# Norm roots by a GpSimd power, and attention heads as three-stage units in a new order, in a two-block transformer kernel

## The chip, the cores and the metric

The kernel runs on one core of one Trainium2 chip. The metric is device time in microseconds (us) of one execution, inputs already in HBM. The core has TensorE (PE, with PEld for its weight loads), VectorE (DVE), ScalarE (ACT), GpSimd (POOL) and SyncE (SP), which issues most of the transfers. Each engine works through its own list of instructions in order.

## What is computed

256 tokens of width 1024 pass two blocks. The first has two layers of: SwiGLU feed-forward, layer norm, hybrid mixer, layer norm, SwiGLU feed-forward, layer norm. The mixer is the part that the change rewrites:

```python
h = split_columns(x @ w_in)                 # 2516 columns for the four mixers
y_a = mla_mixer(...)                        # M: 4 heads, low-rank queries and keys
y_b = nsa_mixer(...)                        # N: 4 heads x (compressed, selected, window)
y_c = dsa_mixer(...)                        # D: top 64 keys by an index score, 4 heads
y_d = stick_breaking_mixer(...)             # S: 4 heads, cumulative sum of log(1 - p)
y = rms_norm(concat(y_a, y_b, y_c, y_d) in 4 groups of 256, group_norm_g)
return y @ w_out
```

The second block (convolution, differential attention, and twice a layer that mixes 16384 experts by product keys) takes the rest of the time, and of it the change touches only the roots of the norms.

## The kernel before

**Layout and products.** Activations lie transposed, 128 of the 1024 features by 256 tokens in a tile. Every large product is made of three passes (`mm3`, L420 to L422): weights and activations are split into a high part in fp32r and the rest, and high by high, high by low and low by high are added in PSUM. `weights` (L391 to L398) brings 128x1024 pieces from HBM by SP, and for each 128x512 half ACT copies the high part (`wh`, L396) and VectorE or GpSimd subtracts it (`wl`, L398). `self.lo` is a string of engines taken in turn; in the mixers it is 'ggv' (two of three on GpSimd), at the head of a mixer or feed-forward `HEAD_LO`, 'g'. The ring has 4 raw pieces and 6 halves of each kind.

**Norms.** A residual sum `x` is written chunk by chunk in `project`, with running sums s1 and s2. `Rows.factors` reduces them with four small matmuls (L300, L301), makes mean and variance (L304 to L306), calls `newton` (L434 to L439: two integer instructions for a first guess and three rounds of three, eleven on VectorE), and `spread` (L445) lays the factors along the rows by PE transposes. So that PE need not wait for this, six input chunks of the mixer (EARLY), or four pairs of the feed-forward, are first computed from the unnormalised sum and corrected later (`normed`). `Rows.finish` then normalises: two VectorE instructions (L324, L325), ACT writes the high part (L328), GpSimd the full value (L329), VectorE the low part (L330). `newton` is also called by the norms inside the mixers (`mla_norm`, and `group_out`, once for each of the four groups) and by those of the second block, 30 times in all.

**Heads.** A head of M, N or D runs through `softmax`: `scores` (L762 and mask matmuls L764, L765, into PSUM bank B), row maxima (L775) and their negative (L777, or L779) on VectorE, exponent on ACT (L782), for N a gate on VectorE (L786, L788), three PE transposes (L791), a copy out of PSUM (L794 on ACT or L796 on VectorE), and then `pv` (L802 to L804), three matmuls into bank D. S has two passes, with all logarithms (L1056) between them. After four heads `group_out` squares, takes the root, scales, transposes (L750) and splits the result (L753, L754).

**Order.** `MIX_ORDER` names the steps, one letter each: b, i, n, d, c, 1, 2 and so on are input chunks and preparations, a and s score and select for D, and M, N, D and S each run one head whole. The layer's order ends `...SSSSSMMMMzsMsknnDDDDNNNNNNDNNNN`. These letters give priorities only: when the program is built, a scheduler fixes each engine's list from them and from estimated durations, and may move an instruction up where its buffers are free. The output product, `project` on `w_out`, follows all heads, eight chunks of 24 matmuls, with the groups in the order in which they end.

Of the kernel before, what the change touches and what calls it, by code (L numbers as in the profile page):

```python
# [15 lines left out]
U32 = mybir.dt.uint32  # L16
# [15 lines left out]
HEAD_LO = 'g'  # L32
HEAD_AT = 1
MIX_LO = ('ggv', 'ggv')
OUT_LO = ('ggv', 'ggv')
FFN_LO = 'v'
MIX_Z = ((), ())
MIX_BANKS = ('A', 'A')
EARLY = 0, 1, 2, 3, 5, 6
MIX_ORDER = ('1bbiciSbvbaaaS2paSduwSdSSSSSMMMMzsMsknnDDDDNNNNNNDNNNN', '1bbiciSbvbaaaS2paSduwSdSSSSSMMMMzsMsnnDDDDkNNNNNNDNNNN')  # L40
# [145 lines left out]
def _layout1(I):  # L186
# [11 lines left out]
    A['w_out'] = _chunked(I['w_out']).reshape(DEPTH, DC, 128, DC * 128)  # L198
# [86 lines left out]
class Rows:  # L285
# [8 lines left out]
    def factors(self, k):  # L294
# [12 lines left out]
        r = k.newton(v)  # L307
# [7 lines left out]
    def finish(self, k):  # L315
# [6 lines left out]
        for c in range(DC):  # L322
# [24 lines left out]
class Kernel:  # L347
    def __init__(self, ctx, nc, tc, I):
# [9 lines left out]
        nc.vector.memset(self.ones, 1.0)  # L358
        self.col = self.tl(gp, [128, 3], "col")
# [69 lines left out]
    def newton(self, v):  # L429

        nc = self.nc
        y = self.tl(self.wk, [128, 8], "ny", bufs=4)[:v.shape[0], :v.shape[1]]
        a = self.tl(self.wk, [128, 8], "na", bufs=4)[:v.shape[0], :v.shape[1]]
        nc.vector.tensor_scalar(y.bitcast(U32), v.bitcast(U32), 1, None, op0=ALU.logical_shift_right)  # L434
        nc.vector.tensor_scalar(y.bitcast(I32), y.bitcast(I32), -1.0, float(0x5f3759df), op0=ALU.mult, op1=ALU.add)
        for _ in range(3):
            nc.vector.tensor_tensor(a, v, y, op=ALU.mult)
            nc.vector.scalar_tensor_tensor(a, a, -0.5, y, op0=ALU.mult, op1=ALU.mult)
            nc.vector.scalar_tensor_tensor(y, a, 1.5, y, op0=ALU.add, op1=ALU.mult)  # L439
        return y  # L440
# [115 lines left out]
    def project(self, src, y, x, scale, eps, gb, out=None, order=None):  # L556
# [14 lines left out]
        for d in range(DC):  # L571
            w = self.weights(src[d], nk)
            ps = self.bank("ACD"[d % 3], T)
            self.linear(ps, w, y, order)
# [45 lines left out]
    def _mixer(self, ctx, l, sm, vec, now, dump):  # L620
# [16 lines left out]
        nf = [0]  # L637

        def fbank(cols):
            nf[0] += 1  # L640
            return self.bank(MIX_BANKS[l][nf[0] % len(MIX_BANKS[l])], cols)

        def fchunk(i, tag=None):

            if i in early:
                t = self.tl(mx, [128, T], tag) if tag else self.tl(mx, [128, 384], "p", bufs=3)[:, :T]
                now.normed(self, t, early[i])
                return t
            z = i in MIX_Z[l]
            ps = fbank(T + 2 if z else T)  # L650
            self.linear(ps, self.weights(win[i], DC), now.z if z else xs)
            if z:
                t = self.tl(mx, [128, T], tag) if tag else self.tl(mx, [128, 384], "p", bufs=3)[:, :T]
                now.normed(self, t, ps)
                return t
            return self.evac(ps, tag) if tag else ps

        def vchunk(name, n, tag):
            w = self.weights(I[name][l], DC, n)
            o = self.tl(mx, [128, 2, n], tag)  # L660
            for t, a in enumerate(TILES):
                ps = fbank(n)
# [7 lines left out]
        def features(n, tag, *chunks):  # L670

            E[n] = []
            for i in chunks:
                E[n].append(fchunk(i, f"{tag}{i}") if tag == "sb" else rope64(i, f"{tag}{i}") if tag == "nq" else rope32(i, f"{tag}{i}"))
                yield

        def once(f):
            f()
            yield
# [29 lines left out]
        def step_u():  # L709
# [4 lines left out]
        later = {  # L714
            'i': lambda: features('iq', "iq", 5, 6), 'n': lambda: features('nq', "nq", 8, 9),
            'd': lambda: features('dq', "nq", 10, 11), 'b': lambda: features('sb', "sb", 12, 13, 14, 15),
            'a': lambda: self.dsa_scores(acc, E['iq'], E['ik'], E['V']), 's': lambda: self.dsa_select(sel, acc),
            'M': lambda: self.mla(E['qkv'], E['kpe']), 'S': lambda: self.stick(E['sb'], lambda: E['sv']),
            'N': lambda: self.nsa(E['nq'], *E['kv'], (E['kk'], E['kx']), (E['kx'], E['kk']), E['V']),
            'D': lambda: self.dsa(E['dq'], (E['m2'], E['m2x']), E['V'], sel),  # L720
            **{n: (lambda f: lambda: once(f))(f) for n, f in zip("c12pwvkzu", (
                step_c, step_1, step_2, step_p, step_w, step_v, step_k, step_z, step_u))}}
        going = {}
        order = MIX_ORDER[l]
        for s in order:
            if s not in going:
                going[s] = later[s]()
            next(going[s], None)
        last = sorted('MNDS', key=order.rindex)

        self.lo = OUT_LO[l]
        return self.project(I['w_out'][l], self.ys, now.x, ALPHA, 1e-5, vec(V_L2G, 16), order=sum([[2 * g, 2 * g + 1] for g in map('MNDS'.index, last)], []))

    def group_out(self, grp, o):
# [9 lines left out]
        r = self.newton(ss)  # L744
        y = self.tl(self.mx, [128, 2, T], "y", bufs=2)
        ps = self.bank("C").rearrange("p (c t) -> p c t", c=2)
        for qc, a in enumerate(TILES):
            nc.vector.tensor_scalar(y[:, qc], o[:, qc], r[:, qc:qc + 1], None, op0=ALU.mult)
            for c in range(2):
                nc.tensor.transpose(ps[:, c, a], y[:, qc, c * 128:c * 128 + 128], self.id1)  # L750
        for c in range(2):
            g, (h, l) = self.vec1(V_GN + 2 * grp + c), self.ys[2 * grp + c]
# [15 lines left out]
    def softmax(self, s, scale, sums, rows=None, eng="v", gate=None):  # L768

        nc, C = self.nc, self.C  # L770
        mm = nc.tensor.matmul
        R = ((0, 128), (128, 384))
        st = self.tl(self.st, [128, 4], "st", bufs=8)
# [6 lines left out]
        p = self.tl(self.mx, [128, 384], "p", bufs=3)  # L780
# [3 lines left out]
        if gate is not None:  # L784
            self.recip(sums)
            nc.vector.tensor_tensor(sums, sums, gate, op=ALU.mult)  # L786
            for qc, (a, b) in enumerate(R):
                nc.vector.tensor_scalar(p[:, a:b], p[:, a:b], sums[:, qc:qc + 1], None, op0=ALU.mult)  # L788
        pt = self.bank("C", 384)
        for i in range(3):  # L790
            nc.tensor.transpose(pt[:, 128 * i:128 * i + 128], p[:, 128 * i:128 * i + 128], self.id1)  # L791
        o = self.tl(self.mx, [128, 384], "pt", bufs=3)
        if eng == "s":
            nc.scalar.activation(o, pt, AF.Copy)  # L794
        else:
            nc.vector.tensor_copy(o, pt)  # L796
        return o

    def pv(self, o0, o1, pt, v, start, stop):
# [11 lines left out]
    def heads(self, g, parts, v, scale, rows=None, masks=()):  # L811

        nc = self.nc
        o = self.bank("D").rearrange("p (q h d) -> p q h d", q=2, h=4)
        sums = self.tl(self.st, [128, 4, 2], "sums", bufs=2)
        for h in range(4):
            pt = self.softmax(self.scores(parts(h), masks), scale, sums[:, h], rows, "sv"[h % 2])
            self.pv(o[:, 0, h], o[:, 1, h], pt, v(h), (h == 0, False), (False, h == 3))
            yield
        self.recip(sums)  # L820
        y = self.tl(self.mx, [128, 2, 4, 64], "o", bufs=2)
        nc.vector.tensor_tensor(y, o, sums.rearrange("p h q -> p q h")[:, :, :, None].to_broadcast([128, 2, 4, 64]), op=ALU.mult)
# [896 lines left out]
```

## Time and profile before

| | us |
|---|---|
| median of 3 runs | 3370.47 (3356.43 to 3370.92) |
| the profiled execution | 3374.15 |
| its span, first to last instruction | 3372.3 |
| first mixer, from its first chunk to its last output chunk | about 200 to 420 |
| second mixer | about 817 to 1026 |

The profile shows one execution. A matmul counts as busy until its modelled end, so PE can read 100% while its matmuls come at half their best rate; the number of matmuls in a stretch and the granted clock (1.00 is 2.4 GHz, 0.50 is 1.2 GHz) tell that. A wait is put to the instruction that ended it.

### The profile page before, as it was taken

To read this page: it belongs to the slowest core of one execution; us is meant where nothing else is said; L and a number is where in the kernel's file an instruction comes from. 1 tells how busy PE (TensorE), PEld (TensorE's weight loads), DVE (VectorE), ACT (ScalarE), POOL (GpSimd) and SP (SyncE) were. 2 spreads that over 40 slices of the span, in tenths; PEclk is the share of its full clock that TensorE was granted. 3 is DMA by queue.
4 is the path that set the end of the run, shared out by engine and by line. 5 is a ranking of instruction groups with operands and counts; after the bars stand their busy time and mean duration, and the time that the engine had idled before them with its cause. 6 is when DMAs were issued, how large, how long until landed. Compare 5 with 4: busy or idle time off the path is not lost.

```text
span 3372.3 us, 70124 instructions
## 1 busy us (share of the span) xinstructions
PE 3205.0 (95%) x27035; PEld 3082.0 (91%) x27035; DVE 2399.8 (71%) x5664; ACT 1650.9 (49%) x3361; POOL 1190.2 (35%) x958
## 2 busy tenths in 40 slices
PE   8989999999999999879999999999988999999998
PEld 8987799999778988879999999999887999999898
DVE  5666576766658579893797548956899397755965
ACT  5555355555535552545444454455454545445444
POOL 0053220303413000565444444344357544444443
PEclk9998799999889999989999999999998999999999
DMA  7642156565205653335444554454344545455454
GB/s 240 183 144 91 45 163 181 165 190 171 82 32 160 184 171 127 121 119 163 151 157 140 168 175 143 141 174 157 102 132 131 185 152 172 156 177 170 132 182 138
DMA packets 140863, 503.16 MB, mean 149 GB/s; under 512 B 17328, under 2 KB 19632, under 8 KB 139888
## 3 DMA queue, kind: packets, MB, share of 16 engines
q1 hardware_dynamic: 137104, 496.06, 46.6%
q8 instruction: 212, 3.47, 0.4%
q10 hardware_dynamic: 3328, 2.36, 0.2%
q14 instruction: 123, 1.01, 0.1%
q0 software_dynamic: 96, 0.26, 0.0%
HBM read 496.36 MB, written 1.05 MB: 147 GB/s over the span
## 4 chain that ended last, share of the span: by engine, by line
PE 51%; DVE 17%; issue 2%; ACT 0%; POOL 0%; DMA 0%; SPq 0%; DVEq 0%; ACTq 0%; POOLq 0%
PE A L420 7%; PE A L421 7%; PE A L422 7%; PE D L420 7%; PE D L422 7%; PE D L421 7%; DVE A L1503 2%; DVE two L1498 2%; DVE wl L398 1%; PE C L1507 1%; PE B L1246 1%; PE C L420 1%; PE C L421 1%; PE C L422 1%; DVE room L1604 1%
## 5 line engine op out<-in xcount | busy, mean ns | idle before, releaser
L396 ACT ACTIVATE wh<-w 128x512 fp32r<-128x512 f32 x1856 | 1152.9, 626 | 1313.7 <-PE A L421 513.4
L398 POOL TENSOR_TENSOR wl<-w,wh 128x512 fp32r<-128x512 f32 x774 | 1069.4, 1389 | 1622.5 <-ACT wh L396 1167.9
L398 DVE TENSOR_TENSOR wl<-w,wh 128x512 fp32r<-128x512 f32 x1082 | 764.3, 708 | 522.4 <-ACT wh L396 482.1
L420 PE MATMUL A<-xh,wh 128*128 128x256 f32 (+2 forms) x1912 | 558.8, 294 | 21.3 <-ACT wh L396 8.7
L421 PE MATMUL A<-xl,wh 128*128 128x256 f32 (+2 forms) x1912 | 556.6, 292 | 9.3 <-DVE xl L330 5.8
L422 PE MATMUL A<-xh,wl 128*128 128x256 f32 (+2 forms) x1912 | 555.1, 291 | 2.8 <-POOL wl L398 2.8
L420 PE MATMUL D<-xh,wh 128*128 128x256 f32 (+2 forms) x1664 | 481.3, 289 | 4.8 <-ACT wh L396 4.4
L422 PE MATMUL D<-xh,wl 128*128 128x256 f32 (+2 forms) x1664 | 477.9, 287 | 7.2 <-DVE wl L398 4.2
L421 PE MATMUL D<-xl,wh 128*128 128x256 f32 (+2 forms) x1664 | 477.9, 287 | 2.1 <-DVE xl L330 2.0
L420 PEld LDWEIGHTS A<-xh,wh 128*128 128x128 f32 x1912 | 370.4, 194 | 25.6 <-ACT wh L396 8.9
L421 PEld LDWEIGHTS A<-xl,wh 128*128 128x128 f32 x1912 | 371.5, 194 | 12.6 <-DVE xl L330 8.0
L422 PEld LDWEIGHTS A<-xh,wl 128*128 128x128 f32 x1912 | 372.6, 195 | 3.8 <-POOL wl L398 3.4
L421 PE MATMUL A<-rr,wh 128*128 128x272 f32 (+1 forms) x1152 | 333.4, 290 | 2.3 <-DVE rr L1196 2.2
L422 PE MATMUL A<-rr,wl 128*128 128x272 f32 (+1 forms) x1152 | 334.2, 290 | 1.1 <-POOL wl L398 1.1
L420 PE MATMUL A<-rr,wh 128*128 128x272 f32 (+1 forms) x1152 | 333.8, 290 | 0.0
L420 PE MATMUL D<-rr,wh 128*128 128x272 f32 (+1 forms) x1152 | 333.4, 289 | 0.0
L422 PE MATMUL D<-rr,wl 128*128 128x272 f32 (+1 forms) x1152 | 333.3, 289 | 0.0
L421 PE MATMUL D<-rr,wh 128*128 128x272 f32 (+1 forms) x1152 | 331.9, 288 | 0.0
L422 PEld LDWEIGHTS D<-xh,wl 128*128 128x128 f32 x1664 | 317.9, 191 | 9.7 <-DVE wl L398 5.6
L420 PEld LDWEIGHTS D<-xh,wh 128*128 128x128 f32 x1664 | 317.9, 191 | 6.7 <-ACT wh L396 5.5
L421 PEld LDWEIGHTS D<-xl,wh 128*128 128x128 f32 x1664 | 317.9, 191 | 3.4 <-DVE xl L330 3.1
L421 PEld LDWEIGHTS A<-rr,wh 128*128 128x128 f32 x1152 | 220.2, 191 | 2.8 <-DVE rr L1196 2.7
(482 smaller groups left out, 6775.2 us busy)
## 6 DMA issues: line engine op xcount, KB each, us to landing
w<-in_u_dram SPq DMA_DIRECT2D x256, 512.0 KB, 3.5
w<-in_v_dram SPq DMA_DIRECT2D x256, 512.0 KB, 3.8
w<-in_ffn_w_dram SPq DMA_DIRECT2D x240, 512.0 KB, 4.1
w<-in_win_f_dram SPq DMA_DIRECT2D x32, 512.0 KB, 3.6
w<-in_f_wq_dram SPq DMA_DIRECT2D x32, 512.0 KB, 3.5
w<-in_ffn_w_dram SPq DMA_DIRECT2D x32, 384.0 KB, 3.2
w<-in_pw_dram SPq DMA_DIRECT2D x24, 512.0 KB, 3.7
w<-in_w_out_dram SPq DMA_DIRECT2D x16, 512.0 KB, 3.7
```

The lines of the kernel that those rows point to most:

```text
L396: nc.scalar.activation(h, s, AF.Copy)
L398: (nc.vector if eng == "v" else nc.gpsimd).tensor_tensor(l, s, h, op=ALU.subtract)
L420: mm(ps, wh, xh, start=start, stop=False)
L421: mm(ps, wh, xl, start=False, stop=False)
L422: mm(ps, wl, xh, start=False, stop=stop)
L1246: mm(pc, d[:, k], u[:, k:k + T2], start=k == 0, stop=k == n - 1)
L1498: nc.vector.tensor_tensor(two, self.key[:, None].to_broadcast([128, 4, 128, 2]), row(1, 128), op=ALU.is_equal)
L1503: nc.vector.tensor_tensor(A[:, i], one, row(2 + i, n), op=ALU.mult)
L1507: mm(ps[:, k], two[:, k // 2, :, k % 2], A[:, i, k // 2, :, k % 2], start=i == 0, stop=i == 1)
L1604: nc.vector.tensor_tensor(c[:, o:o + (b - a) * n].rearrange("p (a b) -> p a b", b=n), r.v[0][:, hd, a:b][:, :, None].to_broadcast([128, b ...
```

## The change

Three things. `newton` becomes `rsqrt`, a single GpSimd power with exponent -0.5. The mixers' and heads' weight splits all go to VectorE, and `finish` leaves GpSimd too (ACT writes the full value and copies the high part from it). And the mixer's heads become generators with a `yield` after the softmax and one after the transposes, which a loop advances: at each `/` of the order every unit under way goes one stage on, after the steps named before that `/`. Input chunks are now named one by one between the heads. Each output chunk can be begun as soon as M and D are done (o0 to o7: rows of groups M and D, which the host has put first) and go on when N is (p0 to p3); `project` then adds the rest. Both layers have the same order.

```diff
-HEAD_LO = 'g'
+HEAD_LO = 'v'
-MIX_LO = ('ggv', 'ggv')
-OUT_LO = ('ggv', 'ggv')
+MIX_LO = ('v', 'v')
+OUT_LO = ('v', 'v')
-MIX_ORDER = ('1bbiciSbvbaaaS2paSduwSdSSSSSMMMMzsMsknnDDDDNNNNNNDNNNN', ...)
+MIX_ORDER = """1 i c i V 2 p / a 7 / a 8 / a 9 w / a 10 s / M 11 s / M 12 z / M 13 / M 14 /
+    D 15 / D C u / D / D / N b / N b / N b / N b / N o0 / N o1 / N o2 / N / L o3 / E / E / E / E p0 p1 / p2 o4 / p3 o5 / o6 / o7"""
+GROUPS = [0, 2, 1, 3]
...
-                nc.scalar.activation(h, q, AF.Identity, bias=b[:, c:c + 1], scale=g[:, c:c + 1])
-                nc.gpsimd.tensor_scalar(o[:, c], q, g[:, c:c + 1], b[:, c:c + 1], op0=ALU.mult, op1=ALU.add)
+                nc.scalar.activation(o[:, c], q, AF.Identity, bias=b[:, c:c + 1], scale=g[:, c:c + 1])
+                nc.scalar.activation(h, o[:, c], AF.Copy)
...
-    def newton(self, v):
+    def rsqrt(self, v):
...
+        nc.gpsimd.tensor_tensor(y, v, self.half[:v.shape[0], :v.shape[1]], op=ALU.pow)
         return y
...
+        if True:
+            for s in MIX_ORDER.split():
+                if s == '/':
+                    old = [g for g in old if next(g, end) is not end] + new
+                    new = []
+                elif s in units:
+                    g = units[s]()
+                    next(g)
+                    new.append(g)
+                else:
+                    steps[s]()
...
+    def out_part(self, pre, src, d, a, b):
+        if d not in pre:
+            if d % 2 == 0:
+                pre['bank'] = self.bank("AADC"[d // 2]).rearrange("p (a t) -> p a t", a=2)
+            pre[d] = SimpleNamespace(ps=pre['bank'][:, d % 2], w=[], done=0)
+        r = pre[d]
+        if b > len(r.w):
+            r.w += self.weights(src[d][:, 512 * (len(r.w) // 4):512 * (len(r.w) // 4) + 512], 4)
+        for k in range(a, b):
+            self.mm3(r.ps, r.w[k], self.ys[k], d % 2 == 0 and k == 0, d % 2 == 1 and k == DC - 1)
+        r.done = b
...
-    def softmax(self, s, scale, sums, rows=None, eng="v", gate=None):
+    def unit(self, qk, masks, scale, sums, v, o, rows=None, eng="v", gate=None):
...
+        yield
         pt = self.bank("C", 384)
         for i in range(3):
             nc.tensor.transpose(pt[:, 128 * i:128 * i + 128], p[:, 128 * i:128 * i + 128], self.id1)
...
+        yield
+        self.pv(*o(), t, v())
```

The tile `p` gets a fourth buffer. In S the units are b (first pass of a head), L (all logarithms) and E (second pass); C is N's compressed branch.

## Rows read from the trace of the kernel before

**Rows 1.** The page's first part: busy us, share of the span, instructions.

```profile
PE 3205.0 (95%) x27035; PEld 3082.0 (91%) x27035; DVE 2399.8 (71%) x5664; ACT 1650.9 (49%) x3361; POOL 1190.2 (35%) x958
```

**Rows 2.** Busy time by stretch, first mixer and the feed-forward's head behind it.

```profile
core 0: us, PE busy (x) PEld busy (x) DVE busy (x) ACT busy (x) POOL busy (x), PEclk, DMA share, GB/s
200.00:223.00 23.00, 19.94 (x155) 19.73 (x154) 16.53 (x36) 10.28 (x18) 16.40 (x19) 0.93 0.42 131
223.00:262.00 39.00, 29.94 (x197) 26.51 (x195) 30.23 (x65) 20.59 (x40) 24.51 (x25) 0.89 0.39 117
262.00:300.00 38.00, 38.00 (x247) 30.14 (x246) 25.96 (x86) 27.15 (x47) 15.12 (x15) 0.98 0.24 73
300.00:331.00 31.00, 31.00 (x193) 24.88 (x192) 17.78 (x58) 10.74 (x34) 9.64 (x11) 0.89 0.18 52
331.00:386.00 55.00, 54.94 (x208) 40.90 (x208) 25.39 (x124) 15.82 (x64) 0.00 (x0) 0.51 0.09 35
386.00:420.00 34.00, 28.37 (x222) 26.56 (x220) 26.30 (x54) 17.03 (x39) 17.64 (x12) 1.00 0.36 108
420.00:465.00 45.00, 40.95 (x290) 39.64 (x291) 35.35 (x90) 28.20 (x55) 20.55 (x19) 0.89 0.47 142
```

**Rows 3.** The same for the second mixer.

```profile
831.00:870.00 39.00, 30.52 (x230) 28.58 (x228) 33.86 (x70) 22.62 (x44) 27.30 (x28) 0.96 0.35 104
870.00:912.00 42.00, 41.05 (x245) 31.56 (x245) 30.90 (x97) 28.81 (x49) 16.06 (x16) 0.92 0.28 92
912.00:949.00 37.00, 36.96 (x223) 29.18 (x221) 18.92 (x63) 12.42 (x40) 9.73 (x11) 0.86 0.15 47
949.00:980.00 31.00, 30.62 (x114) 22.76 (x115) 14.66 (x70) 9.56 (x39) 0.00 (x0) 0.51 0.00 1
980.00:1026.00 46.00, 41.10 (x307) 36.79 (x307) 35.01 (x102) 21.75 (x59) 18.07 (x13) 0.98 0.24 74
```

**Rows 4.** Timeline where D's and N's heads run: start, us, engine, line, operation [idle].

```profile
355.28 0.29 DVE L775 TENSOR_REDUCE st<-B 128x1 f32<-128x128 f32 x1 [1.16 <-PE B L765]
...
355.76 0.37 ACT L782 ACTIVATE p<-B,st 128x128 f32<-128x128 f32 x1 [5.69 <-DVE st L777]
```

**Rows 5.** Timeline of the first mixer's norm: GpSimd, VectorE, PE.

```profile
203.97 7.61 POOL L398 TENSOR_TENSOR wl<-w,wh 128x512 fp32r<-128x512 f32 x6
...
207.81 1.22 DVE L434 TENSOR_SCALAR ny<-lnst 128x2 uint32<-128x2 uint32 x1
...
214.02 0.16 DVE L439 SCALAR_TENSOR_TENSOR ny<-na,ny 128x2 f32<-128x2 f32 x1
...
214.24 0.43 PE L445 MATMUL B<-const,ny 128*128 128x128 f32 x2 [3.06 <-DVE ny L439]
```

**Rows 6.** Waits over the whole run: us in total, times, longest.

```profile
PE B L445 <- DVE ny L439: 26.4, 10, 4.4
```

**Rows 7.** The last norm's root, where GpSimd is idle: first and last of eleven instructions.

```profile
3362.66 0.17 DVE L434 TENSOR_SCALAR ny<-rv 128x2 uint32<-128x2 uint32 x1
...
3364.63 0.16 DVE L439 SCALAR_TENSOR_TENSOR ny<-na,ny 128x2 f32<-128x2 f32 x1
```

**Rows 8.** Small and middle GpSimd instructions: a timeline row, and a group of 200 to 420.

```profile
203.72 0.29 POOL L995 COPY acc<-const 128x128 f32<-128x128 f32 x1
...
L605 POOL TENSOR_TENSOR turn<-turn,const 128x256 f32<-128x256 f32 x10 | 7.6, 764 | 16.7 <-DVE turn L603 16.7
```

**Rows 9.** Weight splits alone (L398), both mixers: DVE busy, POOL busy.

```profile
200.00:420.00 220.00, 12.24 (x15) 58.42 (x43) 0.83 0.26 80
817.00:1026.00 209.00, 14.76 (x15) 56.87 (x44) 0.87 0.24 75
```

**Rows 10.** The page's costliest groups: one split on VectorE, mean ns.

```profile
L398 DVE TENSOR_TENSOR wl<-w,wh 128x512 fp32r<-128x512 f32 x1082 | 764.3, 708 | 522.4 <-ACT wh L396 482.1
```

**Rows 11.** A group of VectorE, 200 to 420: the root's third instruction of a round.

```profile
L439 DVE SCALAR_TENSOR_TENSOR ny<-na,ny 128x2 f32<-128x2 f32 (+1 forms) x18 | 5.7, 319 | 0.5
```

More of the change, by code (lines that the diff above doesn't have):

```diff
@@ L571, in project @@
         for d in range(DC):
-            w = self.weights(src[d], nk)
-            ps = self.bank("ACD"[d % 3], T)
-            self.linear(ps, w, y, order)
+            if d in pre:
+                for i in range(d, d + 2) if d % 2 == 0 else ():
+                    self.out_part(pre, src, i, pre[i].done, nk)
+                ps = pre[d].ps
+            else:
+                ps = self.bank("ACD"[d % 3], T)
+                self.linear(ps, self.weights(src[d], nk), y)
             p = xp[:, d]
@@ L668, in _mixer, with feature @@
         rope32 = lambda i, tag: self.rope(fchunk(i), C_C32, C_S32, tag)
[L670 to L679, printed above, removed]
+        Q = [None] * 16
+        def feature(i):
+            Q[i] = fchunk(i, f"sb{i}") if i > 11 else rope64(i, f"nq{i}") if i > 7 else rope32(i, f"iq{i}")
         def step_c():
@@ L713, in _mixer @@
         sel = self.tl(mx, [128, 384], "sel", BF16)
[L714 to L722, printed above, removed]
@@ L723, in _mixer, with stage @@
-        going = {}
[L724 to L729, printed above, removed]
-        self.lo = OUT_LO[l]
-        return self.project(I['w_out'][l], self.ys, now.x, ALPHA, 1e-5, vec(V_L2G, 16), order=sum([[2 * g, 2 * g + 1] for g in map('MNDS'.index, last)], []))
+        iq = iter((5, 6))
+        going = {}
+        def stage(n, make):
+            if n not in going:
+                going[n] = make()
+            return going[n].pop(0) if isinstance(going[n], list) else next(going[n], None)
@@ new lines, in sticks, with begin @@
+        def sticks(k):
+            if 'S' not in going:
+                going['S'] = self.stick(Q[12:16], lambda: E['sv'])
+            s = going['S'][k]
+            return s.pop(0) if isinstance(s, list) else s
+        pre = {}
+        def begin(i):
+            self.out_part(pre, I['w_out'][l], i, 0, 4)
+        units = {
+            'M': lambda: stage('M', lambda: self.mla(E['qkv'], E['kpe'])),
+            'C': lambda: stage('N', lambda: self.nsa(Q[8:10], *E['kv'], (E['kk'], E['kx']), (E['kx'], E['kk']), E['V'])),
+            'N': lambda: stage('N', None),
+            'D': lambda: stage('D', lambda: self.dsa(Q[10:12], (E['m2'], E['m2x']), E['V'], sel)),
+            'b': lambda: sticks(0), 'L': lambda: sticks(1), 'E': lambda: sticks(2)}
@@ new lines, in _mixer @@
+        steps = {
+            'i': lambda: feature(next(iq)),
+            'a': lambda: stage('a', lambda: self.dsa_scores(acc, Q[5:7], E['ik'], E['V'])),
+            's': lambda: stage('s', lambda: self.dsa_select(sel, acc)),
+            'c': step_c, '1': step_1, '2': step_2, 'p': step_p, 'w': step_w, 'V': step_v, '7': step_k, 'z': step_z, 'u': step_u,
+            **{str(i): (lambda i: lambda: feature(i))(i) for i in range(8, 16)},
+            **{f"o{i}": (lambda i: lambda: begin(i))(i) for i in range(8)},
+            **{f"p{i}": (lambda i: lambda: self.out_part(pre, I['w_out'][l], i, 4, 6))(i) for i in range(4)}}
@@ new lines, in _mixer @@
+        old, new = [], []
+        end = object()
+        if True:
[7 more added lines that the diff above has]
+                    new.append(g)
+                else:
+                    steps[s]()
+        self.lo = OUT_LO[l]
+        return self.project(I['w_out'][l], self.ys, now.x, ALPHA, 1e-5, vec(V_L2G, 16), pre=pre)
@@ L1043, in stick, with first @@
         A, R = [], []
-        for h in range(4):
+        G = SimpleNamespace(o=None)
+        def first(h):
             z = self.bank("B", 384)
```

144 lines of the change are left out of this document (72 added, 72 removed).

## Prediction

> **What bounds the kernel now.** The page comes first: PE is busy for 95% of the span and VectorE for 71% [rows 1], so only time that PE loses can be won. Next come the stretches of the two mixers [rows 2, 3], in which PE's share says little: it reads 54.94 of 55 us at 331 to 386, with only 208 matmuls. I read matmuls per us instead. Where heads of one mixer run beside input chunks, PE gets through 247 in 38 us, 6.5 per us, and behind the heads, with output products, 222 in 34, again 6.5. In the feature stretch (223 to 262) it is 197 in 39, or 5.1. Where the heads of D and N are alone it is 208 in 55, or 3.8, and in the second mixer 114 in 31, or 3.7; the granted clock there is 0.51, so nearly all of it is at 1.2 GHz. A timeline shows why: the row maximum waits 1.16 us for the scores and the exponent 5.69 us for the maxima [rows 4]. The few heads under way go through PE, VectorE and ACT in turn, almost nothing else is left for PE, and there it has the low clock, which makes its next scores later still. In the feature stretch VectorE (30.23 of 39) and GpSimd (24.51) are the busy ones.
>
> Last, the norm at the head of the mixer [rows 5]. GpSimd makes six splits without a pause for 7.61 us, and in just that time VectorE's small instructions take about 1.2 us each, instead of 0.16 when it has stopped. The root ends at about 214.2 and PE has idled 3.06 us for it. Over the run PE waits 26.4 us in ten places for the root's last instruction [rows 6].
>
> **Part 1, roots.** Each of 30 calls loses eleven VectorE instructions, 2.13 us undisturbed (3362.66 to 3364.79) [rows 7], and gains one GpSimd instruction on 2 to 8 columns. No row shows a power. From below the nearest is a GpSimd copy of 128 columns, 0.29 us, from above the root that it replaces, 2.13; a product of 256 columns takes 0.76 [rows 8]. The width is far nearer the first, the function is costlier than a copy: I take 0.5 us. In the heads of the norms the splits leave GpSimd as well, so nothing stands ahead of the power there, and VectorE's few remaining statistics go back from 1.2 to 0.16 us. The chain of rows 5, 8.8 us from the first statistics to the factors, would be some 1.5 us and end before PE comes to it. Where the root was undisturbed, about 1.5 us of 2.13 goes. I leave 0.7 us in each of ten places: 26.4 - 7 = **19 us** gained; the ends are 0 (a power as long as the root) and 26. Behind GpSimd's splits in the second block (still 'g', 'gv' and 'gvv' there) a power may wait for one split, about 1.4 us (58.42 / 43) [rows 9]; the calls there feed results that are needed several heads or chunks later, which hides it. If that cover is gone, it costs eight heads at 1.4 us, 11 us at most.
>
> The Trainium skill (GPSIMD Engine Reference, section "Engine selection") says the opposite of this part: elementwise work on a tile belongs on VectorE, and two-input work on GpSimd takes about twice as long. The splits bear that out, 1.4 us against 0.71 [rows 9, 10]. By that rule the power would pay nothing and the sum would lose its 19 us (a rival below); by rows 5 a VectorE instruction beside GpSimd's work costs up to 1.2 us and eleven of them cost far more than one of any price up to 2 us, so I keep the term.
>
> **Part 2, splits.** 43 splits of the first mixer and 44 of the second leave GpSimd, 58.42 and 56.87 us [rows 9], and cost VectorE 0.71 us each [rows 10], 30 us a mixer. VectorE's busy time from 200 to 420 is 142 us (16.53 + 30.23 + 25.96 + 17.78 + 25.39 + 26.30) [rows 2]. Six roots of eleven instructions, at 0.16 undisturbed [rows 7] to 0.32 as one group has it here [rows 11], take 11 to 21 off. So it has 151 to 161 us, less whatever the collisions of rows 5 cost others. In 187 us that is 81 to 86%: VectorE becomes the second bound, but not the first. Costed at 0 by itself. In the feed-forward's heads (420 to 465) VectorE has 35.35 of 45 [rows 2]; up to 16 splits (11 us) join it and one root leaves, ACT takes over the full value at 28.20 of 45. I cost that at 0, with 5 us either way over three such heads.
>
> **Part 3, head units and order.** No instruction of a head goes. What moves: the transposes of a head stand one stage behind its softmax, its `pv` another, and each of the stages with a, M and D holds an input chunk of 24 matmuls; N's hold S's first passes, then the beginnings of output chunks. So the stretches at 3.8 and 3.7 per us should go at the pace of heads beside chunks. From 223 to 420 there are 1067 matmuls in 197 us, from 831 to 1026 1119 in 195 [rows 2, 3]. At 6.5 per us they take 164 and 172: **33 and 23 us** gained, 56. Two of the ten root waits lie in these stretches, up to 4.4 each [rows 6], so 8 of it is counted already: **48 us**. The ends: at 6.0, the pace of 912 to 949, where heads ran beside few chunks [rows 3], 178 and 187, a gain of 27 less 8, or 19. At 7.8, the pace of 200 to 223 with PE's busy 19.94 us alone (155 matmuls), 137 and 143, a gain of 112 less 8, or 104. I take 6.5, as the new order has both kinds of stretch throughout and N's last stages stay thin. The output weights come in twice as many transfers of half the size on SP's queue, and DMA's share in these stretches is 0.39 at most [rows 2, 3]: 0. What is late next is VectorE: a stage of N has two row maxima, the gate and a logit of S, and there PE will still wait.
>
> **The sum** against the profiled execution of 3374.15 us: 19 + 48 = 67 gives 3307. The median lies 3.7 below that execution, so **3303** (rounded down from 3303.5).
>
> **The rivals.**
> *The pace does not change.* The builder's scheduler already moved later scores up between heads, and the stages write out what it did. For it: 262 to 300 already runs at 6.5 without the new stages. Against it: in the thin stretches no input chunk was left to move up. Only the roots pay: 3370 - 19 = 3351.
> *The power is slow,* as long as a root or longer: its 19 us are gone, 3370 - 48 = 3322. For it: the rule cited in part 1, and that no row has a power. Against it: 2 to 8 columns.
> *The clock holds everywhere.* Chunks between all heads keep PE at 2.4 GHz, and it runs at 7.8 per us: 3370 - 19 - 104 = 3247. Against it: four N stages hold no chunk at all.
> *Slower: VectorE's list.* All splits, maxima, gates and copies stand in one list in order. If a split (0.71) stands ahead of each of the 32 row maxima of a mixer's 16 such heads, each head's chain is later by 1.4 us, 23 us a mixer, with nothing behind it to fill PE; less the roots' 19, that is +27: 3397. For it: in 831 to 870 VectorE already has 33.86 of 39 and PE 30.52 [rows 3]. It decides once VectorE is busy for over 90% of a stretch with heads. The Trainium skill (TensorE: Matmul & The Clock Gate, section "Architectural detail") gives the rule behind this, that VectorE and ACT take their queues strictly in order; rows 4 agree, where ACT's exponent idles behind one wait.
>
> **How the numbers follow.** The forecast has 0.52, the slow power 0.06, the unchanged pace 0.15, the clock that holds 0.13, the slower case 0.14. About 0.5% (17 us) is what a measurement of this kernel can tell from no change, that is 3353.6 to 3387. Forecast, slow power and clock are faster (0.71), the unchanged pace at 3351 lies on that edge and half of it counts as faster (0.07), half as same; of the slower case 0.02 ends within. So 0.78, 0.10, 0.12. The range: 3247 below; above, the unchanged pace with a slow power, 3370: 3245 to 3372. It leaves the slower case out and a little below.
>
> **What would show it.** Right: the wait of PE for the root gone from the waits (L445, under 8 us in all); VectorE's 1.2 us statistics gone; the low clock in the mixers under 40 us where it was 86 in the two thin stretches alone; over 6 matmuls per us from the first feature to the last output chunk; VectorE at 80 to 86% there. Wrong: a power above 2 us; row maxima that start late although their scores have ended (VectorE busy, not waiting for PE); thin stretches as long as before with clock 0.5.

## The result and the profile after

The changed kernel takes 3315.35 us (median of 4 runs, 3311.29 to 3319.97) against 3365.65 for the kernel before on the same chip: a ratio of 0.9846 [0.9817, 0.9875], 1.5% less, or 52 us by that ratio (the two medians are 50 apart). Here and below, a difference in us is worked out from the ratio, and the brackets are its 95% interval. The forecast was 67 us less, so the direction and the range held. The composition did not: the parts that were to pay little paid nearly all, and the part that was to pay most paid nothing. The profiled run took 3316.61 us, span 3314.7.

The page's first part after, which answers to [rows 1]:

```profile
PE 3170.8 (96%) x27035; PEld 3057.0 (92%) x27035; DVE 2333.2 (70%) x5464; ACT 1665.5 (50%) x3401; POOL 1007.5 (30%) x819
```

The reader sees that VectorE (DVE) is busy for 67 us less than before, although it took over splits from GpSimd (POOL), which has 139 instructions less, its 30 powers counted. The roots that left VectorE are the larger part of it: with the roots alone it is 90 us less, with the splits alone still 3 us less (e1 and e2 below). Next the stretches of both mixers, which answer to [rows 2, 3]; the first mixer now ends at about 396, the second runs from 785 to 980.

```profile
core 0: us, PE busy (x) PEld busy (x) DVE busy (x) ACT busy (x) POOL busy (x), PEclk, DMA share, GB/s
201.00:223.00 22.00, 21.52 (x181) 21.30 (x179) 17.73 (x46) 14.13 (x27) 2.61 (x6) 1.00 0.52 162
223.00:258.00 35.00, 27.59 (x156) 23.15 (x154) 26.17 (x67) 17.74 (x39) 14.35 (x17) 0.76 0.24 75
258.00:300.00 42.00, 42.00 (x272) 35.91 (x271) 30.27 (x107) 15.44 (x38) 7.25 (x9) 0.88 0.35 120
300.00:331.00 31.00, 31.00 (x205) 23.89 (x204) 17.30 (x61) 18.51 (x52) 0.71 (x1) 1.00 0.17 52
331.00:352.00 21.00, 18.31 (x74) 12.76 (x73) 10.72 (x41) 16.06 (x36) 0.73 (x1) 0.59 0.00 0
352.00:397.00 45.00, 44.55 (x327) 40.50 (x327) 23.26 (x64) 21.35 (x54) 1.39 (x2) 0.96 0.31 95
...
807.00:842.00 35.00, 27.39 (x154) 22.90 (x153) 26.07 (x65) 17.46 (x39) 14.44 (x18) 0.76 0.25 74
842.00:884.00 42.00, 42.00 (x272) 36.24 (x270) 30.14 (x106) 15.88 (x39) 6.81 (x9) 0.88 0.24 78
884.00:914.00 30.00, 29.54 (x202) 23.37 (x201) 16.51 (x58) 16.88 (x49) 0.71 (x1) 1.00 0.16 49
914.00:938.00 24.00, 24.00 (x84) 16.71 (x84) 12.46 (x43) 17.81 (x39) 0.70 (x1) 0.51 0.00 1
938.00:980.00 42.00, 41.50 (x314) 37.35 (x314) 22.23 (x63) 20.55 (x53) 1.39 (x2) 1.00 0.32 101
```

Three things are to be read here. From the first feature to the last output chunk PE does 1034 matmuls in 174 us (223 to 397) and 1026 in 173, 5.9 per us. The thin stretch (331 to 352, 3.5 per us, clock 0.59) is short where it was 55 us long in the first mixer [rows 2]; whether the order did that is seen under e2. And a new weak stretch stands at the start, 223 to 258: 4.5 matmuls per us and clock 0.76, where the kernel before did 5.1 at 0.89 [rows 2]. Time at the low level is twice (1 - clock) of a stretch: 17, 10, 17 and 4 us in the first mixer, 48 together, and 51 in the second. By the same sum [rows 2, 3] have 74 and 52.

The norm at the head of the mixer, VectorE's timeline and then GpSimd's (start, us, engine, line, operation, idle before); they answer to [rows 5]:

```profile
207.41 0.15 DVE L305 COPY lnst<-B 128x4 f32<-128x4 f32 x1
207.60 0.16 DVE L306 TENSOR_TENSOR lnst<-lnst 128x2 f32<-128x2 f32 x1
207.79 0.16 DVE L307 SCALAR_TENSOR_TENSOR lnst<-lnst 128x2 f32<-128x2 f32 x1
...
208.98 0.15 DVE L309 SCALAR_TENSOR_TENSOR lnst<-lnst,ny 128x2 f32<-128x2 f32 x1
```

```profile
208.03 0.71 POOL L436 TENSOR_TENSOR ny<-lnst,half 128x2 f32<-128x2 f32 x1 [4.85 <-DVE lnst L307]
```

The statistics take 0.16 us instead of 1.2, the power 0.71, and from the start of the statistics (L305) to that of the last factor (L309) it is 1.6 us. All powers on that line, two of the forms (count, shortest, median and longest in ns), and over the whole run the time that PE waited for them (us, times), which answers to [rows 6]:

```profile
L436 POOL TENSOR_TENSOR ny<-ss,half x8: 695/696/730, 316.6 to 962.8; 128x2 f32<-128x2 f32 x8
...
L436 POOL TENSOR_TENSOR ny<-mst,half x2: 1017/1020/1022, 243.5 to 827.0; 128x4 f32<-128x4 f32 x2
...
  PE B L442: 6.4, 4
```

### The profile page after: what moved, and what is told of

The parts are those of the page before. It is cut to its first block, busy times and chain, and to the rows that moved or that the text cites. A ratio compares the mean times of both kernels' runs of the same rounds, so it can differ in the third digit from the quotient of the medians.

```text
span 3314.7 us, 69729 instructions
## 1 busy us (share of the span) xinstructions
PE 3170.8 (96%) x27035; PEld 3057.0 (92%) x27035; DVE 2333.2 (70%) x5464; ACT 1665.5 (50%) x3401; POOL 1007.5 (30%) x819
## 4 chain that ended last, share of the span: by engine, by line
PE 74%; DVE 18%; issue 5%; ACT 2%; DMA 1%; POOL 0%; ACTq 0%; SPq 0%; POOLq 0%; DVEq 0%
PE A L423 10%; PE A L424 10%; PE A L425 10%; PE D L423 9%; PE D L425 8%; PE D L424 8%; PE C L423 3%; PE C L424 3%; PE C L425 3%; DVE two L1561 2%; DVE A L1566 2%; DVE wl L401 2%; PE B L795 1%; PE C L1570 1%; DVE room L1667 1%
## 5 line engine op out<-in xcount | busy, mean ns | idle before, releaser
L399 ACT ACTIVATE wh<-w 128x512 fp32r<-128x512 f32 (+1 forms) x1856 | 1156.1, 626 | 1317.4 <-PE A L424 512.8
L401 DVE TENSOR_TENSOR wl<-w,wh 128x512 fp32r<-128x512 f32 (+1 forms) x1212 | 864.7, 715 | 564.8 <-ACT wh L399 546.7
L401 POOL TENSOR_TENSOR wl<-w,wh 128x512 fp32r<-128x512 f32 x644 | 891.5, 1390 | 978.4 <-ACT wh L399 938.7
L423 PEld LDWEIGHTS D<-rr,wh 128*128 128x128 f32 x1152 | 220.6, 192 | 0.0
```

What stands on the lines that cost most here:

```text
L399: nc.scalar.activation(h, s, AF.Copy)
L401: (nc.vector if eng == "v" else nc.gpsimd).tensor_tensor(l, s, h, op=ALU.subtract)
L423: mm(ps, wh, xh, start=start, stop=False)
```

## The experiments

Each part of the change was made alone, in pairs, and with one wait taken away. Ratios are to the kernel before, which ran at 3362 to 3366 us beside them. The stages of each profile are cut at the last write of `x` in `project` (us); the first feed-forward, 199 to 202 us in all of them, is left out:

| version | ratio [95%] | mixer 1 | mixer 2 | three feed-forwards | second block |
|---|---|---|---|---|---|
| before | | 218.8 | 208.4 | 596.8 | 2148.2 |
| e1 roots | 0.9920 [0.9893, 0.9947] | 220.4 | 204.3 | 581.9 | 2127.6 |
| e2 splits | 0.9913 [0.9879, 0.9947] | 195.2 | 194.1 | 592.3 | 2137.1 |
| e3 roots, splits | 0.9853 [0.9829, 0.9878] | 197.7 | 203.3 | 583.8 | 2124.7 |
| e4 order | 1.0007 [0.9993, 1.0022] | 213.0 | 211.8 | 600.1 | 2142.5 |
| changed kernel | 0.9846 [0.9817, 0.9875] | 194.6 | 194.9 | 587.6 | 2136.1 |
| e5 copies by SP | 0.9799 [0.9774, 0.9824] | 192.2 | 189.2 | 590.6 | 2129.3 |
| e6 chunks in front | 0.9854 [0.9819, 0.9889] | 191.2 | 194.4 | 590.2 | 2132.2 |
| e7 mixers' splits | 0.9960 [0.9938, 0.9982] | 209.0 | 207.1 | 595.0 | 2149.6 |
| e8 heads' splits | 0.9951 [0.9933, 0.9970] | 204.9 | 211.5 | 588.6 | 2143.9 |
| e9 = e3, copies by SP | 0.9850 [0.9827, 0.9873] | 198.8 | 200.9 | 583.8 | 2129.5 |
| e10 = e5 and e6 | 0.9847 [0.9823, 0.9871] | 197.0 | 196.8 | 593.4 | 2125.0 |
| e11 = e5, later `u` | 0.9805 [0.9783, 0.9827] | 187.5 | 192.5 | 591.0 | 2129.4 |
| e12 no early products | 0.9889 [0.9863, 0.9915] | 203.9 | 200.1 | 583.0 | 2130.1 |

A ratio of 0.001 is 3.4 us. A stage is one execution: the second block, whose instructions no order of the mixers touches, reads 2125 to 2136 among the versions with the power, so single stages are read with several us of doubt. A profiled execution can also lie off its median: that of e7 is 12 us above, that of e12 7 us below.

### The three parts, each alone

**e1, the roots alone**, in the kernel before:

```diff
-    def newton(self, v):
+    def rsqrt(self, v):
...
+        nc.gpsimd.tensor_tensor(y, v, self.half[:v.shape[0], :v.shape[1]], op=ALU.pow)
```

> The kernel before with the GpSimd power for the roots and nothing else: splits stay on GpSimd at the heads of the norms and two of three in the mixers. Theory A (the parts add, each by its own term): about 19 us less than before, ratio 0.994, PE's wait for the root's last instruction from 26 us to under 8. Theory B (the roots pay because the splits leave GpSimd): the power waits behind up to one split of 1.4 us and the statistics on VectorE stay at 1.2 us, so 5 to 10 us less, ratio 0.997 to 0.9985.

Measured: 3333.96 us, 27 us less (18 to 36), nearer to theory A's 19 than to theory B's 5 to 10. PE's wait for the root is 2.5 us instead of 26.4:

```profile
PE B L441 <- POOL ny L435: 2.5, 2, 1.4
```

So the power need not have GpSimd to itself. At the head of the first mixer the statistics still take 1.1 to 1.2 us, as theory B has it, but the power runs between two splits and PE waits no longer. The table says where the time went: hardly in the mixers (+1.6, -4.1), but in the feed-forwards (-15) and the second block (-21). The last holds beyond the scatter: the five versions with the VectorE root have it at 2137 to 2150 (mean 2144), the nine with the power at 2125 to 2136 (mean 2129), which is 15 us for its 14 roots, of 20 if each gave what it saves by itself (2.13 [rows 7] less 0.70, 1.43 us). In the mixers GpSimd's splits still stand; its groups from 200 to 421 (busy us, mean ns | idle before):

```profile
L400 POOL TENSOR_TENSOR wl<-w,wh 128x512 fp32r<-128x512 f32 (+1 forms) x44 | 59.2, 1362 | 63.8 <-ACT wh L398 58.0 <-PE A L423 5.4
...
L435 POOL TENSOR_TENSOR ny<-ss,half 128x2 f32<-128x2 f32 x4 | 2.8, 704 | 40.7 <-DVE ss L739 40.7
```

**e2, the splits alone**, in the kernel before:

```diff
-HEAD_LO = 'g'
+HEAD_LO = 'v'
-MIX_LO = ('ggv', 'ggv')
-OUT_LO = ('ggv', 'ggv')
+MIX_LO = ('v', 'v')
+OUT_LO = ('v', 'v')
...
-                nc.scalar.activation(h, q, AF.Identity, bias=b[:, c:c + 1], scale=g[:, c:c + 1])
-                nc.gpsimd.tensor_scalar(o[:, c], q, g[:, c:c + 1], b[:, c:c + 1], op0=ALU.mult, op1=ALU.add)
+                nc.scalar.activation(o[:, c], q, AF.Identity, bias=b[:, c:c + 1], scale=g[:, c:c + 1])
+                nc.scalar.activation(h, o[:, c], AF.Copy)
```

> The kernel before with the splits of heads and mixers on VectorE and the full value of the norms by ACT; roots by eleven VectorE instructions, old order. Theory A: no change within 5 us either way. Theory B: the collisions of small VectorE instructions with GpSimd's splits go, so the roots take 2.1 us instead of up to 9 and the feature stretches get shorter: 15 to 25 us less. A third, the slower rival of the prediction (VectorE's list is full): 10 us or more slower.

Measured: 3326.33 us, 29 us less (18 to 41), which theory B expected (15 to 25), and the mixers are 24 and 14 us shorter in the old order. VectorE's groups say why. First those of the kernel before from 200 to 420 (busy us, mean ns | idle before), then those of e2 from 200 to 397:

```profile
L398 DVE TENSOR_TENSOR wl<-w,wh 128x512 fp32r<-128x512 f32 x14 | 11.4, 818 | 9.5 <-issue 5.7 <-ACT wh L396 3.8
L580 DVE SCALAR_TENSOR_TENSOR xl<-x,vec,xh 128x256 fp32r<-128x256 f32 x8 | 6.9, 863 | 0.0
...
L330 DVE TENSOR_TENSOR xl<-x,xh 128x256 fp32r<-128x256 f32 x8 | 5.4, 679 | 0.6 <-POOL x L329 0.5
...
L439 DVE SCALAR_TENSOR_TENSOR ny<-na,ny 128x2 f32<-128x2 f32 x15 | 4.8, 318 | 0.4
...
L324 DVE TENSOR_TENSOR lnt<-x,B 128x256 f32<-128x256 f32 x8 | 3.3, 413 | 1.2 <-ACT rows L313 1.2
```

```profile
L398 DVE TENSOR_TENSOR wl<-w,wh 128x512 fp32r<-128x512 f32 x55 | 39.3, 723 | 10.4 <-ACT wh L396 8.8 <-PE B L445 0.8 <-PE C L421 0.7
...
L580 DVE SCALAR_TENSOR_TENSOR xl<-x,vec,xh 128x256 fp32r<-128x256 f32 x7 | 3.4, 483 | 0.0
L330 DVE TENSOR_TENSOR xl<-x,xh 128x256 fp32r<-128x256 f32 x8 | 3.3, 418 | 0.2 <-ACT xh L329 0.2
L324 DVE TENSOR_TENSOR lnt<-x,B 128x256 f32<-128x256 f32 x8 | 3.3, 414 | 0.0
...
L439 DVE SCALAR_TENSOR_TENSOR ny<-na,ny 128x2 f32<-128x2 f32 x15 | 2.4, 158 | 0.3
```

The splits on VectorE rise from 11.4 to 39.3 us, and instructions with two inputs in SBUF that ran beside GpSimd's splits take less, many of them half: 863 to 483 ns, 679 to 418, 318 to 158. L324, whose second input is a PSUM bank (B), stays at 413 and 414. Over the mixer VectorE is busy for 139 us (200 to 397) where it was 142: it took 28 us of work over and got 31 back. Over the whole run it has 130 instructions more than before [rows 1] and is busy for 3 us less:

```profile
PE 3175.7 (96%) x27035; PEld 3054.1 (92%) x27035; DVE 2396.5 (72%) x5794; ACT 1664.6 (50%) x3401; POOL 985.7 (30%) x788
```

A rival would be that GpSimd's splits, twice as long, simply came too late for PE. PE waits for one of them only 0.6 us in the first mixer of before and 1.1 in the second, so that is not the direct cause. The shorter times show again in e2's wait for the root, which is still VectorE's eleven instructions there: 8.5 us where [rows 6] had 26.4.

```profile
PE B L445 <- DVE ny L439: 8.5, 7, 2.8
```

The row maxima of the heads (first and last start) show where the mixer won: in the kernel before and in e2.

```profile
L775 DVE TENSOR_REDUCE st<-B x32: 290/352/419, 302.5 to 381.5; 128x1 f32<-128x128 f32 x16, 128x1 f32<-128x256 f32 x16
```

```profile
L775 DVE TENSOR_REDUCE st<-B x32: 291/354/420, 291.3 to 363.8; 128x1 f32<-128x128 f32 x16, 128x1 f32<-128x256 f32 x16
```

The maxima begin 11 us earlier and take 72.5 us instead of 79, without a change to the heads' order. These two account for 18 of the 24 us. The windows of e2's first mixer show the thin stretch:

```profile
200.00:223.00 23.00, 21.30 (x176) 20.89 (x175) 18.20 (x53) 12.99 (x24) 1.89 (x5) 1.00 0.55 159
223.00:262.00 39.00, 35.93 (x247) 29.00 (x246) 33.23 (x87) 28.79 (x61) 11.73 (x14) 1.00 0.39 119
262.00:300.00 38.00, 38.00 (x235) 30.86 (x233) 27.05 (x96) 23.28 (x44) 5.55 (x6) 0.91 0.17 57
300.00:331.00 31.00, 30.54 (x182) 23.94 (x181) 18.51 (x68) 11.51 (x40) 3.89 (x5) 0.83 0.31 112
331.00:352.00 21.00, 21.00 (x80) 16.07 (x81) 9.37 (x44) 4.65 (x19) 0.00 (x0) 0.50 0.00 0
352.00:397.00 45.00, 42.01 (x303) 37.92 (x302) 32.80 (x115) 22.69 (x61) 0.00 (x0) 0.94 0.24 71
```

The low clock, which lasted to 386 before, ends soon after 352 here, in the old order. Time at the low level falls from 74 to 44 us, which at the full level would save about 15 (an estimate from the two levels), and PE's idle time from 17.8 us [rows 2] to 8.2: together the 24. The changed kernel has 48 us at the low level, so its shorter thin stretch is no mark of the order.

**e7 and e8** divide e2: the mixers' own splits (`MIX_LO`, `OUT_LO`) in e7, the heads of the norms (`HEAD_LO`, and `finish` on ACT) in e8, each by the lines of e2's diff that bear on it.

> The kernel before with only the mixers' own splits and those of the output product on VectorE (two strings), heads of norms still on GpSimd. If the gain of the splits (36 us alone) comes from taking GpSimd's 1.4 us splits out of the mixers' products: 20 to 30 us less than before, ratio 0.991 to 0.994. If it comes from the heads of the norms, where six splits in a row stretch the root and the normalisation: under 8 us less.

> The kernel before with only the splits at the heads of norms on VectorE and the norms' full value by ACT; mixers' splits stay two of three on GpSimd. If the heads of the norms carry it: 20 us or more less than before, ratio under 0.994, with the root in 2.1 us and PE's wait for it under 10 us in all. If the mixers' products do: 5 to 12 us less.

Measured: 3350.77 us, 13 less (6 to 21), and 3349.02 us, 16 less (10 to 23); PE's wait for the root is 15.8 and 13.1 us. Each lies between what its two theories expected (the 36 us named there is the plain difference of the medians of e2, 29 by the ratio). Their sum is e2's 29: neither half does it alone, and neither undoes the other.

**e3, roots and splits in the old order** (the diffs of e1 and e2 together), and **e4, the order alone** (the changed kernel with `newton`, the old strings of engines and the old `finish`):

```diff
-HEAD_LO = 'v'
+HEAD_LO = 'g'
-MIX_LO = ('v', 'v')
-OUT_LO = ('v', 'v')
+MIX_LO = ('ggv', 'ggv')
+OUT_LO = ('ggv', 'ggv')
...
-    def rsqrt(self, v):
+    def newton(self, v):
```

> Both of these, with the old heads and order. Theory A: 19 us less than before, so 33 us of the whole change's 52 belong to the order. Theory B: 25 to 30 us less, and the order is worth 22 to 27.

> The changed kernel with its new heads, order and early output products, but roots by eleven VectorE instructions, splits two of three on GpSimd in the mixers and all at the heads of norms, the norms' full value by GpSimd. Theory A: the order's own term, about 33 us less than before. Theory B: the order keeps GpSimd's splits in the way of its short stages and pays half of that, 10 to 20 us less.

Measured: e3 3311.33 us, 0.9853; e4 3366.14 us, 1.0007. The two agree: the old order with roots and splits is as fast as the whole change (0.9846), and the new order without them gains nothing. e3 gained more than either theory had, e4 less than either. The terms of e1 and e2 add to 56, e3 has 49, within their intervals.

### Where the order's gain went

In the changed kernel the stretch 223 to 258 was the weak one. Waits from 201 to 260 (us, times, longest), and ACT's timeline there:

```profile
ACT lnt L343 <- DMA ik<-m: 6.1, 1, 6.1
...
PE D L880 <- ACT p L874: 5.5, 1, 5.5
```

```profile
230.00 2.53 ACTq L614 DMA_DIRECT2D kpe<-m  x4
...
232.56 2.54 ACTq L614 DMA_DIRECT2D ik<-m  x4
235.14 0.60 ACT L343 ACTIVATE lnt<-rows,zcol 128x256 f32<-128x256 f32 x1 [6.12 <-DMA ik<-m]
...
235.31 0.52 ACTq L614 DMA_DIRECT2D vx<-m  x1
```

`copies` issues thirteen transfers a mixer on ACT's queue, nine of them here. Eight stand in a row, 0.63 us each, ahead of the squares (L874) that PE needs for the norm inside the mixer (L880). ACT executes nothing for 6.12 us: about 1 us until GpSimd has written the tile `m` that is copied, then 5.1 us for the eight. PE waits 5.5. In the old order PE had other chunks there; e3's waits from 200 to 300 have for the same pair

```profile
PE D L834 <- ACT p L827: 0.7, 1, 0.7
```

The copies hold ACT there too: in e3's second mixer its squares wait 5.2 us for them, and PE waits 1.7.

Theory G: this new wait eats what the order wins. Theory H: the order wins nothing anyway. **e5** lets SP issue all of them, in the changed kernel; **e9** does the same in e3's old order, where G expects nothing of it.

```diff
-            self.nc.scalar.dma_start(t[at:at + src.shape[0]], src)
+            self.nc.sync.dma_start(t[at:at + src.shape[0]], src)
```

> The changed kernel with the copies of keys between partitions (kpe, ik, vx, m2x, kx) issued from SP's queue in place of ACT's. Theory G (given back: the new order gains in the head stages and loses it at the start of each mixer, where nine transfers on ACT's queue hold ACT for 6.1 us, PE waits 5.5 us behind it and has the low clock for 17 us, with no stick-breaking chunk in front to cover it): 10 us or more a layer comes back, so about 20 us less than the changed kernel, ratio to before 0.978 to 0.980, and the low clock in the mixers down from 48 and 51 us to about 31 and 34. Theory H (the head stages gain nothing themselves): within 5 us of the changed kernel, ratio 0.983 to 0.986; the wait is replaced by another in the same place.

> The old heads, order and late output product, with the power roots, all splits on VectorE and the key copies issued by SP: the changed kernel with copies by SP, less its order. Theory G (the order pays once its new wait is taken away): the copies' queue matters little in the old order, which had stick-breaking chunks in front of it, so this stays at the 0.985 it has with copies by ACT (0.983 to 0.987), and the order is worth 10 to 20 us beside the 0.980 of the new order with copies by SP. Theory H (the order pays nothing in itself): this comes down as the new order did, to 0.979 to 0.982.

Measured: e5 3300.68 us, 0.9799; e9 3316.86 us, 0.9850. The edit is worth 16 us in the new order (the interval of the difference, from the two intervals, 3 to 28) and nothing in the old one. So with SP's copies the order, early output products included, is worth 17 us (6 to 29; 0.9850 against 0.9799, their intervals don't meet). Windows of e5:

```profile
223.00:258.00 35.00, 30.45 (x151) 24.68 (x151) 25.54 (x64) 17.66 (x38) 14.35 (x18) 0.71 0.23 68
258.00:300.00 42.00, 42.00 (x295) 35.91 (x294) 31.92 (x112) 16.93 (x44) 7.44 (x9) 0.96 0.37 126
...
805.00:840.00 35.00, 31.20 (x195) 26.57 (x196) 30.32 (x72) 19.70 (x42) 17.96 (x21) 0.85 0.31 93
```

PE's idle time in the weak stretch falls from 7.4 to 4.6 us, and in the second mixer from 7.6 to 3.8; the stretch behind it does 295 matmuls where it did 272. The mixers are 2.4 and 5.7 us shorter. That is half of the 16; the other half lies in stages that the edit doesn't touch, within the doubt of one execution. In the first mixer the clock of the weak stretch stayed low (0.71), and the time at the low level is 47 us where G expected 31; in the second it fell to 38 (34 expected). G holds in its direction; its size in the mixers is nearer 8 than 16.

**e6** fills the hole instead: two input chunks of M's stages go to the front. **e10** is e6 with e5's edit.

```diff
-MIX_ORDER = """1 i c i V 2 p / a 7 / a 8 / a 9 w / a 10 s / M 11 s / M 12 z / M 13 / M 14 /
+MIX_ORDER = """1 12 13 i c i V 2 p / a 7 / a 8 / a 9 w / a 10 s / M 11 s / M z / M / M 14 /
```

> The changed kernel with two stick-breaking input chunks (12, 13) moved from between M's heads to the start of the order, ahead of the first rotary step and of c, as cover for the wait at the start of the mixer; everything else stays. Theory G: PE has 5.6 us of matmuls beside the nine transfers, the wait of 5.5 us goes and the low clock with it; M's stages lose two of their chunks, which costs less than that: 5 to 15 us less than the changed kernel, ratio 0.980 to 0.983. Theory H: no change within 5 us, or slower where M's stages become thin.

> The changed kernel with both: key copies by SP, and input chunks 12 and 13 moved to the start of the order. If the start of the mixer is still short of work for PE (two low-clock pieces of 10 us each remain there in the first mixer): another 5 to 10 us, ratio 0.977 to 0.979. If moving chunks forward only makes the later stages thin: no change or up to 5 us slower than 0.980.

Measured: e6 3316.35 us, 0.9854, no change against the changed kernel; e10 3316.57 us, 0.9847, so with SP's copies the shift costs 16 us (4 to 28). In e6 PE's wait of 5.5 us is gone in both mixers (0.8 is left), and still nothing is won. The windows of e10 suggest the reason: the head of the mixer is now at full clock, and the stages of M are thin in both layers.

```profile
223.00:258.00 35.00, 31.46 (x223) 26.28 (x224) 32.91 (x76) 22.55 (x50) 16.05 (x19) 1.00 0.39 117
...
300.00:335.00 35.00, 35.00 (x160) 25.44 (x158) 16.50 (x61) 17.60 (x49) 0.71 (x1) 0.65 0.08 24
...
885.00:915.00 30.00, 29.80 (x132) 21.83 (x131) 13.89 (x52) 13.49 (x43) 0.71 (x1) 0.62 0.12 36
```

160 matmuls in 35 us are 4.6 per us at clock 0.65, where the changed kernel did 205 in 31 at 1.00. The chunks move the low clock; there were too few to keep it away in both places.

**e11** takes `u`, the step behind C, from D's stages into N's, with e5's edit:

```diff
-    D 15 / D C u / D / D / N b / N b / N b / N b / N o0 / N o1 / N o2 / N / L o3 / E / E / E / E p0 p1 / p2 o4 / p3 o5 / o6 / o7"""
+    D 15 / D C / D / D / N b / N b u / N b / N b / N o0 / N o1 / N o2 / N / L o3 / E / E / E / E p0 p1 / p2 o4 / p3 o5 / o6 / o7"""
```

> The changed kernel with key copies by SP, and the largest chunk of the mixer, the values of S (u, 48 matmuls), moved from D's second stage into the third stage of N, which holds no chunk and has the low clock for 24 us in each layer. If thin stages and their clock are what eats the order's gain: 5 to 10 us less than with copies by SP, low clock in the mixers from 48 and 38 us to under 35 and 25. If the scheduler moves the chunk up anyway, or VectorE and ACT bound N's stages: no change within 4 us.

Measured: 3300.66 us, 0.9805, the same as e5. The first mixer is 4.7 us shorter, with 34 us at the low level instead of 47, the second 3.3 longer, with 46 instead of 38. The shift is not worth anything that the total shows.

**e12** takes the early output products out of the changed kernel:

```diff
-    D 15 / D C u / D / D / N b / N b / N b / N b / N o0 / N o1 / N o2 / N / L o3 / E / E / E / E p0 p1 / p2 o4 / p3 o5 / o6 / o7"""
+    D 15 / D C u / D / D / N b / N b / N b / N b / N / N / N / N / L / E / E / E / E / / / /"""
```

> The changed kernel (copies by ACT) without early output products: o0 to o7 and p0 to p3 are dropped and project computes every output chunk whole behind the last head. If they fill N's and S's thin stages: each mixer is longer by 5 us or more, 3325 us or above, ratio 0.988 or more. If the scheduler moved output products up by itself, as the trace of before shows with four output chunks finished together at the end of the heads: no change within 5 us.

Measured: 3327.84 us, 0.9889, 14 us slower than the changed kernel (1 to 28), and the mixers are 9.3 and 5.2 us longer. The thin stretch of N, in the windows of e12:

```profile
336.00:372.00 36.00, 32.78 (x120) 24.11 (x120) 13.21 (x56) 16.03 (x43) 0.73 (x1) 0.53 0.00 0
```

It lasts 36 us at 3.3 matmuls per us where the changed kernel has 21. So the early products do what they are for, and the rest of the order (units and chunks in new places, copies on ACT) is about 12 us worse than the old one (0 to 24; 0.9889 against 0.9853): the two cancel. A little of the early products' gain seems to be given back behind the mixers: the feed-forward that follows takes 197.6 to 200.3 us and 198.8 to 201.6 (first and second layer) in the five versions with the power that have them, 195.0 to 195.1 and 196.5 to 196.7 in e3, e9 and e12, 2 to 5 us each.

## Why the prediction was right and wrong

The total (-67 forecast, -52 measured) came near by luck, through errors that cancel: roots -19 forecast, -27 alone; splits 0, -29 alone; order -48, 0.

**Part 1 was right in its mechanism and mis-sized.** The wait went from 26.4 to 6.4 us, 20 gained where 19 was forecast; the 1.2 us statistics are gone; a power of 0.70 us (1.02 with four columns) lies near the 0.5 taken. But e2 removed 18 of those 26 us with the old root in place: either edit takes most of it away, so it belonged to the splits beside the root as much as to the root. That the splits leave GpSimd, on which the prediction built, was not needed: e1 has 2.5 us of it with the splits in place. The step that was mis-sized is the one put at nothing, that the calls of the second block are hidden because their results are needed "several heads or chunks later": they gave about 15 us there. The slow power did not come to pass: one GpSimd instruction of 0.70 us beat eleven of VectorE, 2.13.

**Part 2's "costed at 0 by itself" failed.** The prediction read in [rows 5] that GpSimd's splits stretch VectorE's instructions sevenfold, and used it for the norm alone; elsewhere it wrote "less whatever the collisions of rows 5 cost others" and left that unpriced. VectorE was forecast at 81 to 86% of the mixer; it has 125 of 196 us, 64% (the sum of DVE in the first six windows after). No stage of a mixer has VectorE above 81%, so the slower rival had no place.

The Trainium skill (SBUF — State Buffer, section "Who interferes with whom") states the rule: a VectorE instruction with two SBUF inputs and a GpSimd instruction that reads SBUF cannot run together, one blocks for the whole of the other. The trace agrees: beside splits of 7.61 / 6 = 1.27 us the two-input statistics took 1.2 us, and the two-input groups shown under e2 fell when the splits had left, while L324, with an input from PSUM, did not.

**Part 3's 48 us failed**, at the step "At 6.5 per us they take 164 and 172". The pace taken from one good stretch was laid over the whole mixer; after, it is 5.9, and 6.1 with SP's copies (1057 matmuls from 223 to 397). The mixers did become 24 and 14 us shorter (33 and 23 forecast), but not by the order: e2 has them at 195.2 and 194.1 us in the old order, as short as the whole change, and e4 at 213.0 and 211.8 with the new order alone. Three things stood against the order. Copies that the old order covered now stopped ACT, and through it PE, at the head of the mixer; the prediction looked at the transfers of the output weights only, not at those of `copies`, which the new order moves closer to the squares. The new order holds the same number of chunks, and moving two of them forward left the stretch that they came from thin (e10). And these two took up what the early output products won (14 us, e12).

The signs that it named: the wait under 8 us, right (6.4); low clock under 40 us in the mixers, wrong (48, and 51 in the second; the 86 beside it was that of the two thin stretches alone, and the whole mixers had 74 and 52); over 6 per us, wrong (5.9); VectorE at 80 to 86%, wrong (64%); power under 2 us, right.

Of the other rivals, the unchanged pace had the order's worth right (nothing) and left out the splits' gain. Its reason, that the stages write out what the scheduler did already, does not fit: e12 and e5 show an order that wins in one place and loses in another. The clock that holds everywhere did not come: of 126 us at the low level in both mixers 99 are still there.

**What stays open.** Why the clock stays low at the head of the first mixer in e5 (0.71), why e5 gains and e6, which takes away the same wait of PE, does not, and what else in N's last stages would fill PE. e8 moves the heads' splits and changes `finish` in one edit, and no run parts the two. The mixers of the changed kernel are 11 us shorter than e3's in the two profiles and the totals are equal; 4 of that is in the feed-forwards, the rest in the second block's scatter, which single profiles can't resolve. The fastest versions run are e5 and e11, 3301 us, 0.980, faster than both kernels.

## What to carry to other kernels

When two engines share a path, price the collisions for every instruction that runs beside them: moving work onto the busier engine can leave it less busy. A new order has to be read for what it uncovers as well as for what it fills, transfers issued on a compute engine's queue first of all. A pace taken from one full stretch does not carry over to a whole phase in which the number of filler chunks has not changed. And each part of a change has to be run alone before the total is put down to one of them.

## What was not expected of the hardware

- Splits on VectorE cost it less than nothing: 28 us of them joined in the first mixer and its busy time fell by 3 (e2), since its own instructions had been stretched while GpSimd's 43 splits of 1.4 us ran.
- Even an instruction with one input, L434 on integers, took 1.22 us beside the splits [rows 5], where it takes 0.17 undisturbed [rows 7].
- A copy issued from ACT's queue cost ACT 0.63 us, and eight in a row held it for 5.1 us; from issue to landing such a copy took 1.9 us (median). The Trainium skill (DMA: Bandwidth & Descriptors, section "Issuing engines are not separate DMA queues") calls the sequencer's time for a transfer usually small beside the transfer itself; here it was a third of it, and issuing from SP was worth about 16 us of the kernel in the new order (3 to 28, e5; 8 of it in the mixers) and nothing in the old one (e9).
- A GpSimd power on 128x2 takes 0.70 us, near what a product of 128x256 takes there (0.76 [rows 8]). Its time grows with the columns: 0.87 us was the shortest on three, 1.02 the median on four, about 0.16 us a column.
